# Holding weight splits back around two transposing stages of a decoder block, and moving the forget gate behind the first

## The chip, the core and the metric

The kernel runs on one core of a Trainium2 chip. The metric is the time of one execution on the device in microseconds, as the median of several runs. Traces come from one profiled execution on the same core.

## The reference

One hybrid decoder layer on 256 tokens of width 1024, in float32. Cut to its order:

```python
h = rms_norm(x, attn_norm_g)
qa, ka, va, qb, kb, vb, f_logit, g_logit = split(h @ w_in)     # 512 wide each, then 8, then 2048
qa, ka = partial_rope(rms_norm(heads(qa))), partial_rope(rms_norm(heads(ka)))
o_a = moba_attention(qa, ka, heads(va))       # 256 tokens are one block: causal softmax, 8 heads of 64
qb, kb = rms_norm(heads(qb)), rms_norm(heads(kb))
c = cumsum(log_sigmoid(f_logit + b_forget))   # the forget gate, one number per head and token
o_b = softmax(qb @ kb.T / 8 + c[t] - c[s], causal) @ heads(vb)
gates = sigmoid(g_logit + b_gate)
x = x + (gates[0] * (o_a @ w_branch_moba) + gates[1] * (o_b @ w_branch_fox)) @ w_out
u, g = split(rms_norm(x) @ w_ffn_up)
x = x + (silu(causal_conv(g)) * u) @ w_ffn_down
```

## The kernel before

**Split products.** Every large product is made of three: both operands are split into a high part in fp32r and a low part (value minus high part), and high x high, low x high and high x low are summed in one PSUM bank. Weights arrive in *chunks* of 128x2048 by one DMA each (L130, on SP's queue, into `raw`, three buffers) and are split in *halves* of 128x1024: the high part `whi` is a copy on ScalarE (L137), the low part `wlo` a subtraction on VectorE (L138). `whi` and `wlo` have six buffers each (`HB`). The raw buffer is free when the low part of its second half is made; a `whi`/`wlo` buffer is free when TensorE has used it.

**The order of the halves** is the list `units`: the eight `head` pieces (moba q and k), then "qkv" 1 (fox q, four halves), "qkv" 2 (fox k, four), "wg" 0 and 1 (two each), "qkv" 0 (moba v, four), "wg" 2, "qkv" 3 (fox v), "wg" 3 to 7, then "wb", "wo", "wu" and "wd". `use(c, h)` is called when TensorE's code comes to a half; it first emits the splits up to `AHEAD` = 5 halves further on (`load`), then hands out the half.

**What sets the order on the engines.** TensorE's order is the order of the code. On the other engines a planner orders instructions at compile time by its own picture of when each is ready and by a rank, which is the place in the code; inside `with soon(offset)` the rank is that many instructions earlier (`SOON` = 45, `FIRST` = 160). `after(i, j)` makes the planner put `i` behind `j`; on one engine this is an order alone, with no semaphore. PSUM has eight banks, taken by tile (`bank()`), and a bank is free when the instruction that reads it out is done.

**The two stages.** In TensorE's order:

1. `project(3)`, `project(4)` (fox q and fox k): 12 matmuls for each half. `finish_qk` follows each: squares on ScalarE (L308), sums per head on VectorE (L309), an inverse root in small steps (`rsqrt_mean`, L220 to L224, with two ScalarE steps at L221), and the scaling of q or k out of the bank (L321, one instruction for each 128 tokens).
2. `gate(0)`: 48 matmuls (L531 to L533) for one 128-wide column of both merge gates; VectorE takes it out of its bank (L541).
3. `turn_qk` four times (moba q, moba k, fox q, fox k): sixteen transposes each into two banks (L348), copied out by ScalarE (L353). `forget_a` stands ahead of the fourth: sixteen small products (L369), a high part on ScalarE (L370), a low part on VectorE (L371). `forget_b` sums its four strips by two more matmuls (L379) that stand behind the first three matmuls of the second half of `gate(1)`.
4. `gate(1)`, the moba scores and softmax, the moba v projection, `gate(2)`, the fox scores and softmax, the fox v projection, `gate(3)` to `gate(5)`.
5. `turn(0)` and `turn(1)`: 48 transposes each for the probabilities of the two branches (L483), into six banks each, copied out by six ScalarE copies each (L487). `last_exp[0]` is then the last of these twelve copies; the sigmoids of the gates (L545) are put behind it.
6. `gate(6)`, `values()` (probabilities times v, L501; copies of the result L517 and their low parts L518), `gate(7)`, then the branch products ("wb", L629 to L631), `w_out` and the feed-forward part.

Of the kernel before, what the change touches and what calls it, by code (L numbers as in the profile page):

```python
# [8 lines left out]
F32 = mybir.dt.float32  # L9
# [3 lines left out]
ALU = mybir.AluOpType  # L13
# [4 lines left out]
P = 128  # L18
S = 256
NT = 2  # L20
D = 1024
KT = D // P
HD = 64
NH = 8
# [6 lines left out]
RB, HB, AHEAD = 3, 6, 5  # L31
# [13 lines left out]
def decoder_block(ctx, tc, a, out):  # L45
    nc = tc.nc
# [6 lines left out]
    def T(shape, tag, bufs=1, dt=F32):  # L53
        return sb.tile(shape, dt, tag=tag, bufs=bufs, name=tag)
# [4 lines left out]
    def bank():  # L59
        return ps.tile([P, 512], F32, tag="bank", bufs=8, name="bank")  # L60
# [5 lines left out]
    def T16(n, tag, dt=F32R):  # L66
        t = T([P, n * S + 64], tag, 1, dt)
        return t[:, 4:4 + n * S].rearrange("p (k t) -> p k t", k=n)
# [24 lines left out]
    pos = {u: i for i, u in enumerate(units)}  # L93
# [1 line left out]
    loads = {}  # L95
    rs_done = []
    first_lo = []
    state = {"next": 0, "raw": None}

    def after(i, j):  # L100
        tc.add_manual_dep(i.ins, j.ins.name, mybir.DependencyInfo(mybir.DependencyClass.NoSync, mybir.DependencyReason.DATA), reason="order")

    def load(upto):
        while state["next"] <= min(upto, len(units) - 1):
            c, h = units[state["next"]]
            if c[0] == "head":
                k = c[1]
                if k < 2:
                    raw = gates[:, 4 * k:4 * k + 4].rearrange("p a b t -> p (a b t)")
                    for s0, s1 in ((0, HX + W4), (HX + W4, HEADW)):  # L110
                        loads[c] = nc.sync.dma_start(raw[:, s0:s1], a["head"][k][:, s0:s1])
                    x, g, raw = raw[:, 0:S], raw[:, S:S + 1], raw[:, HX:HEADW]
                    nc.gpsimd.tensor_copy(xT[:, k], x)
                else:
                    if k % 2 == 0:
                        state["raw"] = T([P, 2048], "raw", RB)
                    raw = state["raw"][:, k % 2 * 1024:(k % 2 + 1) * 1024]
                    x, g = xT[:, k], g1[:, k:k + 1]
                    nc.sync.dma_start(x, a["head"][k][:, 0:S])
                    loads[c] = nc.sync.dma_start(raw, a["head"][k][:, HX:HEADW])  # L120
                xlo = split_x(k, x, g)
                at, n = 44, 2 if k < 2 else 1
            else:
                at, n = 44 if c[0] == "qkv" else 0, 1
                if h == 0:
                    src = a[c[0]]
                    for j in c[1:]:
                        src = src[j]
                    state["raw"] = T([P, 2048], "raw", RB)
                    loads[c] = nc.sync.dma_start(state["raw"], src)  # L130
                raw = state["raw"][:, h * 1024:(h + 1) * 1024]
            hi = T([P, 1088], "whi", HB, F32R)[:, at:at + 1024]
            lo = T([P, 1088], "wlo", HB, F32R)[:, at:at + 1024]
            w = 1024 // n
            for j in range(n):
                s = slice(j * w, (j + 1) * w)
                i = nc.scalar.activation(hi[:, s], raw[:, s], AF.Copy)  # L137
                d = nc.vector.tensor_tensor(lo[:, s], raw[:, s], hi[:, s].bitcast(F32), op=ALU.subtract)  # L138
                if (c, h) == (("qkv", 1, 1), 0):
                    after(i, rs_done[0])  # L140
                    after(d, rs_done[1])
                if (c, h) == (("qkv", 1, 0), 0):
                    first_lo.append(d)
                if c[0] == "head" and j == 0:
                    after(d, xlo)
            if c[0] == "head":
                square_x(k, x, i)
            split[c, h] = (hi, lo)
            state["next"] += 1

    def use(c, h):
        load(min(pos[c, h] + AHEAD, KT + 1) if c[0] == "head" else pos[c, h] + AHEAD)
        return split.pop((c, h))


# [76 lines left out]
    flat = T16(4, "aT")  # L232
# [47 lines left out]
    def project(m, pt, h, between=None):  # L280
        for hh in range(2):
            if hh and between:
                between()
            wh, wl = use(("qkv", m - 2, h), hh)
            turns = [(k2, i, t) for k2 in range(2) for i in range(3) for t in range(NT)]
            if h == 0 and hh == 0:
                turns.sort(key=lambda x: x[2])
            for k2, i, t in turns:
                k = 4 * h + 2 * hh + k2
                c = slice(k2 * 512, (k2 + 1) * 512)  # L290
                lhs, rhs = ((xh, wh), (xl, wh), (xh, wl))[i]
                nc.tensor.matmul(pt[t], lhs[:, k, t * P:(t + 1) * P], rhs[:, c], start=(k == 0 and i == 0), stop=(k == KT - 1 and i == 2))  # L292
# [9 lines left out]
    def finish_qk(br, pts):  # L302
        n = len(pts)
        ss = T([P, 2, NT, NH], "ss", 2)[:, 0:n]
        for m, (isk, pt) in enumerate(pts):
            for t in range(NT):
                sq = T([P, W4], "sq", 2)
                nc.scalar.activation(sq, pt[t], AF.Square, scale=rs[:, t:t + 1])  # L308
                nc.vector.tensor_reduce(ss[:, m, t], sq.rearrange("p (h d) -> p h d", h=NH), axis=AX.X, op=ALU.add)  # L309
        f = T([P, 2, NT, NH], "qf", 2)[:, 0:n]  # L310
        rsqrt_mean(f.rearrange("p m t h -> p (m t h)"), ss.rearrange("p m t h -> p (m t h)"), HD, [n * NT * NH], "qfv")
        nc.vector.tensor_tensor(f, f, rs[:, None, :, None].to_broadcast([P, n, NT, NH]), op=ALU.mult)
        qns = []
        for m, (isk, pt) in enumerate(pts):
            if br == 0:
                qn = T([P, NT, NH, HD], "qn", 2)
            else:
                qn = qn1[:, 4 * isk:4 * isk + 4].rearrange("p k t -> p (k t)").rearrange("p (t h d) -> p t h d", t=NT, h=NH)
            qns.append(qn)
            for t in range(NT):  # L320
                nc.vector.tensor_tensor(qn[:, t], pt[t].rearrange("p (h d) -> p h d", h=NH),  # L321
                                        f[:, m, t, :, None].to_broadcast([P, NH, HD]), op=ALU.mult)
            if br == 0:
                rc, rsn = rope[isk]
                p1 = T([P, NT, NH, 16], "p1", 1)
                p2 = T([P, NT, NH, 16], "p2", 1)
                x16 = qn[:, :, :, 0:16]
                nc.gpsimd.tensor_tensor(p1, x16, rc[:, :, None, :].to_broadcast([P, NT, NH, 16]), op=ALU.mult)
                nc.gpsimd.tensor_tensor(p2, x16, rsn[:, :, None, :].to_broadcast([P, NT, NH, 16]), op=ALU.mult)
                nc.gpsimd.tensor_tensor(qn[:, :, :, 0:8], p1[:, :, :, 0:8], p2[:, :, :, 8:16], op=ALU.add)  # L330
                nc.gpsimd.tensor_tensor(qn[:, :, :, 8:16], p1[:, :, :, 8:16], p2[:, :, :, 0:8], op=ALU.add)
        return qns
# [32 lines left out]
    def forget_a():  # L365
        fp = bank()
        for k in range(KT):
            r = slice(32 * (k % 4), 32 * (k % 4 + 1))
            nc.tensor.matmul(fp[r, :S], wfg[:, k], xT[:, k], start=(k < 4), stop=(k >= 4))  # L369
        nc.scalar.activation(flat[:, 0], fp[:, :S], AF.Copy)  # L370
        nc.vector.tensor_tensor(flat[:, 1], fp[:, :S], flat[:, 0].bitcast(F32), op=ALU.subtract)  # L371

    def row(i):
        return gates[:NH, 4 + i // 2, i % 2]
# [51 lines left out]
    last_exp = []  # L426
# [110 lines left out]
    def gate(c, between=None):  # L537
        gp = bank()
        twin("wg", c, gp, xh, xl, between=between)
        with soon(FIRST):  # L540
            return nc.vector.tensor_tensor(gates[:, c], gp.rearrange("p (b t) -> p b t", b=2), rsB[:, None, :].to_broadcast([P, 2, S]), op=ALU.mult)  # L541
# [10 lines left out]
    def banks():  # L552
        return [bank() for _ in range(NT)]
# [11 lines left out]
        qkn = finish_qk(0, ((0, pq), (1, pk)))  # L565
    for isk in range(2):
        pt = banks()
        project(3 + isk, pt, 0)
        project(3 + isk, pt, 1)
        with soon(FIRST):  # L570
            qkn += finish_qk(1, ((isk, pt),))
    gate(0)
    with soon():
        for i, qn in enumerate(qkn):
            if i == 3:
                forget_a()
            turn_qk(qn, i // 2, i % 2)

    def between():
        with soon():  # L580
            forget_b()
# [21 lines left out]
    finish_v(pv, 1)  # L603
    gate(3)
    gate(4)
    gate(5)
    with soon():
        turn(0)
        last_exp[:] = [turn(1)]
    gate(6)  # L610
    oh, ol, copied = values()
    gate(7)
# [206 lines left out]
```

## Time and profile before

| | us |
|---|---|
| median of 3 runs | 366.54 (366.1 to 366.68) |
| the profiled execution | 364.58 |
| its span, first to last instruction | 362.8 |
| TensorE busy | 354.6 (98%) |
| VectorE busy | 274.4 (76%) |
| ScalarE busy | 218.0 (60%) |

In the profile PE is TensorE, PEld its weight loads, DVE VectorE, ACT ScalarE, POOL GpSimd, SP the engine whose queue issues the DMAs; L138 is line 138 of the kernel. A timeline row has start and duration in us, engine, line, operation, the tiles it writes and reads (out<-in), the shapes and how many instructions are merged in it; in brackets stands the idle time of the engine ahead of it, and what ended that idle time.

### The profile page before, as it was taken

To read this page: it belongs to the slowest core of one execution; us is meant where nothing else is said; L and a number is where in the kernel's file an instruction comes from. 1 tells how busy PE (TensorE), PEld (TensorE's weight loads), DVE (VectorE), ACT (ScalarE), POOL (GpSimd) and SP (SyncE) were. 2 spreads that over 40 slices of the span, in tenths; PEclk is the share of its full clock that TensorE was granted. 3 is DMA by queue.
4 is the path that set the end of the run, shared out by engine and by line. 5 is a ranking of instruction groups with operands and counts; after the bars stand their busy time and mean duration, and the time that the engine had idled before them with its cause. 6 is when DMAs were issued, how large, how long until landed. Compare 5 with 4: busy or idle time off the path is not lost.

```text
span 362.8 us, 7564 instructions
## 1 busy us (share of the span) xinstructions
PE 354.6 (98%) x3119; PEld 337.7 (93%) x3119; DVE 274.4 (76%) x483; ACT 218.0 (60%) x363; POOL 34.2 (9%) x51
## 2 busy tenths in 40 slices
PE   8999998999997999999999999999999999999995
PEld 5888897888897999999999999999999999999995
DVE  5899795899998267985979876768676866768643
ACT  5858657595695987544778545546455545546420
POOL 3432080320000000000530000000000000000000
PEclk9999999999999999999999999999999999999999
DMA  8987666326338433664555654554655554554003
GB/s 287 402 304 252 228 228 233 116 118 234 116 117 314 153 117 126 224 210 154 220 161 195 227 207 149 224 195 164 226 196 168 218 207 155 218 191 161 1 2 116
DMA packets 12131, 68.29 MB, mean 188 GB/s; under 512 B 1688, under 2 KB 2848, under 8 KB 4672
## 3 DMA queue, kind: packets, MB, share of 16 engines
q1 hardware_dynamic: 11664, 66.62, 51.1%
q0 software_dynamic: 288, 1.19, 0.8%
q8 instruction: 24, 0.39, 0.4%
q14 instruction: 11, 0.09, 0.1%
q10 hardware_dynamic: 144, 0.00, 0.0%
HBM read 66.75 MB, written 1.06 MB: 187 GB/s over the span
## 4 chain that ended last, share of the span: by engine, by line
PE 94%; DVE 2%; DMA 1%; issue 1%; ACT 1%; DVEq 0%
PE bank L531 15%; PE bank L533 15%; PE bank L532 14%; PE bank L292 12%; PE bank L278 6%; PE bank L733 6%; PE bank L732 5%; PE bank L731 5%; PE bank L657 2%; PE bank L631 2%; PE bank L656 2%; PE bank L655 2%; PE bank L630 2%; PE bank L629 2%; PE bank L501 1%; PE bank L440 1%
## 5 line engine op out<-in xcount | busy, mean ns | idle before, releaser
L138 DVE TENSOR_TENSOR wlo<-raw,whi 128x1024 fp32r<-128x1024 f32 x120 | 147.4, 1231 | 50.6 <-ACT whi L137 50.4
L137 ACT ACTIVATE whi<-raw 128x1024 fp32r<-128x1024 f32 x120 | 125.8, 1057 | 78.0 <-PE bank L532 42.0
L533 PE MATMUL bank<-oh,wlo 128*128 128x256 f32 x352 | 96.8, 275 | 0.0
L531 PE MATMUL bank<-oh,whi 128*128 128x256 f32 x352 | 96.8, 275 | 0.0
L532 PE MATMUL bank<-ol,whi 128*128 128x256 f32 x352 | 96.8, 275 | 0.0
L531 PEld LDWEIGHTS bank<-oh,whi 128*128 128x128 f32 x352 | 66.1, 188 | 0.0
L533 PEld LDWEIGHTS bank<-oh,wlo 128*128 128x128 f32 x352 | 66.1, 188 | 0.0
L532 PEld LDWEIGHTS bank<-ol,whi 128*128 128x128 f32 x352 | 66.1, 188 | 0.0
L531 PE MATMUL bank<-xh,whi 128*128 128x256 f32 x128 | 35.6, 278 | 0.0
L533 PE MATMUL bank<-xh,wlo 128*128 128x256 f32 x128 | 35.2, 275 | 0.0
L532 PE MATMUL bank<-xl,whi 128*128 128x256 f32 x128 | 35.2, 275 | 0.0
L531 PEld LDWEIGHTS bank<-xh,whi 128*128 128x128 f32 x128 | 24.0, 188 | 0.3
L532 PEld LDWEIGHTS bank<-xl,whi 128*128 128x128 f32 x128 | 24.0, 188 | 0.1
L533 PEld LDWEIGHTS bank<-xh,wlo 128*128 128x128 f32 x128 | 24.0, 188 | 0.0
L292 PE MATMUL bank<-whi,xh 128*128 128x512 f32 x64 | 21.2, 391 | 0.0
L292 PE MATMUL bank<-whi,xl 128*128 128x512 f32 x64 | 21.0, 388 | 0.0
L292 PE MATMUL bank<-wlo,xh 128*128 128x512 f32 x64 | 21.0, 388 | 0.0
L698 DVE TENSOR_TENSOR sq<-bank,rs 128x512 f32<-128x512 f32 x22 | 15.1, 691 | 6.6 <-PE bank L533 6.5
L629 PE MATMUL bank<-oh,whi 128*128 128x256 f32 x64 | 17.6, 275 | 0.0
L630 PE MATMUL bank<-ol,whi 128*128 128x256 f32 x64 | 17.6, 275 | 0.0
L631 PE MATMUL bank<-oh,wlo 128*128 128x256 f32 x64 | 17.6, 275 | 0.0
L655 PE MATMUL bank<-xh,whi 128*128 128x256 f32 x64 | 17.6, 275 | 0.0
(200 smaller groups left out, 749.5 us busy)
## 6 DMA issues: line engine op xcount, KB each, us to landing
raw<-in_wu SPq DMA_DIRECT2D x22, 1024.0 KB, 4.8
raw<-in_wd SPq DMA_DIRECT2D x11, 1024.0 KB, 4.8
raw<-in_qkv SPq DMA_DIRECT2D x8, 1024.0 KB, 4.9
raw<-in_wg SPq DMA_DIRECT2D x8, 1024.0 KB, 4.8
raw<-in_wb SPq DMA_DIRECT2D x4, 1024.0 KB, 5.3
raw<-in_wo SPq DMA_DIRECT2D x4, 1024.0 KB, 4.9
raw<-in_head SPq DMA_DIRECT2D x6, 512.0 KB, 6.6
gates<-cd POOLq DMA_DIRECT2D x1, 1024.0 KB, 4.5
```

The lines of the kernel that those rows point to most:

```text
L137: i = nc.scalar.activation(hi[:, s], raw[:, s], AF.Copy)
L138: d = nc.vector.tensor_tensor(lo[:, s], raw[:, s], hi[:, s].bitcast(F32), op=ALU.subtract)
L278: nc.tensor.matmul(pt[t], lhs[:, k, t * P:(t + 1) * P], rhs, start=(k == 0 and i == 0), stop=(k == KT - 1 and i == 2))
L292: nc.tensor.matmul(pt[t], lhs[:, k, t * P:(t + 1) * P], rhs[:, c], start=(k == 0 and i == 0), stop=(k == KT - 1 and i == 2))
L531: nc.tensor.matmul(o, wh[:, w], mh[:, k], start=(k == 0 and i == 0), stop=False)
L532: nc.tensor.matmul(o, wh[:, w], ml[:, k], start=False, stop=False)
L533: nc.tensor.matmul(o, wl[:, w], mh[:, k], start=False, stop=(k == KT - 1 and i == 1))
L629: nc.tensor.matmul(o, wh[:, w], oh[:, 4 * br + k], start=(k == 0), stop=False)
L630: nc.tensor.matmul(o, wh[:, w], ol[:, 4 * br + k], start=False, stop=False)
L631: nc.tensor.matmul(o, wl[:, w], oh[:, 4 * br + k], start=False, stop=(k == 3))
L655: nc.tensor.matmul(o, wh[:, w], mh[:, k], start=(k == 0 and i == 0), stop=False)
L733: nc.tensor.matmul(o, wl[:, w], ah, start=False, stop=(last and h == 1 and d == ds[-1]))
```

## The change

`state` gains a `lag`: for halves behind the `head` pieces `use` emits splits up to `AHEAD - lag` halves further on. `catch_up(lag, hi, lo)` sets a new lag and at once emits the halves that the smaller lag allows (one half at each of its three calls); `hi` and `lo` name instructions behind which the high and the low parts of these halves are put. The lag is 2 in `project(4)`; behind it one half is emitted with its low part behind k's last scaling (L321), and the lag is 1 through `gate(0)`. `forget_a` moves behind the fourth `turn_qk`; behind it one half is emitted with its low part behind the forget gate's low part (L371), and the lag is 0. In `gate(5)` the lag is 1 again; behind `turn(1)` one half is emitted with its high part behind the last copy of the turned probabilities (L487). No instruction is added or removed.

```diff
-    state = {"next": 0, "raw": None}
+    state = {"next": 0, "raw": None, "lag": 0, "hi": None, "lo": None}
...
                 if c[0] == "head" and j == 0:
                     after(d, xlo)
+                for this, last in ((i, state["hi"]), (d, state["lo"])):
+                    if last is not None:
+                        after(this, last)
...
+    def catch_up(lag=0, hi=None, lo=None):
+        upto = state["next"] - 1 + state["lag"] - lag
+        state.update(lag=lag, hi=hi, lo=lo)
+        load(upto)
+        state.update(hi=None, lo=None)
+
     def use(c, h):
-        load(min(pos[c, h] + AHEAD, KT + 1) if c[0] == "head" else pos[c, h] + AHEAD)
+        load(min(pos[c, h] + AHEAD, KT + 1) if c[0] == "head" else pos[c, h] + AHEAD - state["lag"])
...
-                nc.vector.tensor_tensor(qn[:, t], pt[t].rearrange("p (h d) -> p h d", h=NH),
-                                        f[:, m, t, :, None].to_broadcast([P, NH, HD]), op=ALU.mult)
+                state["qn"] = nc.vector.tensor_tensor(qn[:, t], pt[t].rearrange("p (h d) -> p h d", h=NH),
+                                                      f[:, m, t, :, None].to_broadcast([P, NH, HD]), op=ALU.mult)
...
-        nc.vector.tensor_tensor(flat[:, 1], fp[:, :S], flat[:, 0].bitcast(F32), op=ALU.subtract)
+        return nc.vector.tensor_tensor(flat[:, 1], fp[:, :S], flat[:, 0].bitcast(F32), op=ALU.subtract)
...
         pt = banks()
+        state["lag"] = 2 * isk
         project(3 + isk, pt, 0)
         project(3 + isk, pt, 1)
         with soon(FIRST):
             qkn += finish_qk(1, ((isk, pt),))
+    catch_up(lag=1, lo=state["qn"])
     gate(0)
     with soon():
         for i, qn in enumerate(qkn):
-            if i == 3:
-                forget_a()
             turn_qk(qn, i // 2, i % 2)
+        flat_lo = forget_a()
+    catch_up(lo=flat_lo)
...
     gate(4)
+    state["lag"] = 1
     gate(5)
     with soon():
         turn(0)
         last_exp[:] = [turn(1)]
+    catch_up(hi=last_exp[0])
     gate(6)
```

## The prediction

> **What bounds the kernel now.** I read the page's summary, then TensorE's own waits, then the timelines of TensorE, VectorE and ScalarE around each wait, and one piece of the chain that ended last.
>
> ```profile
> span 362.8 us, 7564 instructions
> PE 354.6 (98%) x3119; PEld 337.7 (93%) x3119; DVE 274.4 (76%) x483; ACT 218.0 (60%) x363; POOL 34.2 (9%) x51
> ```
>
> TensorE is busy 354.6 of 362.8 us. The change takes no matmul away, so all it can win is idle TensorE time, 8.2 us at most. Who ends that idle time (columns: total us, times, longest):
>
> ```profile
> PE bank L483 <- DVE gates L541: 1.9, 1, 1.9
> PE bank L348 <- DVE gates L541: 0.7, 1, 0.7
> PE bank L348 <- DVE ol L321: 0.4, 1, 0.4
> ```
>
> All three stand at transposes: L483 turns the probabilities, L348 turns q and k. VectorE ends them: twice by L541, which empties a gate's bank, once by L321, which scales k. The first stage on TensorE (start us, us):
>
> ```profile
> 54.17 1.21 PE L348 MATMUL bank<-cst,qn 64*128 64x64 f32 x32
> 55.22 0.22 PE L348 MATMUL bank<-cst,ol 64*128 64x64 f32 x1
> 56.17 0.71 PE L348 MATMUL bank<-cst,ol 64*128 64x64 f32 x15 [0.72 <-DVE gates L541]
> 56.80 1.07 PE L369 MATMUL bank<-xT,wfg 128*32 128x256 f32 x16
> 58.29 0.97 PE L348 MATMUL bank<-cst,ol 64*128 64x64 f32 x16 [0.41 <-DVE ol L321]
> 59.19 0.38 PE L531 MATMUL bank<-xh,whi 128*128 128x256 f32 x1
> ```
>
> From 54.17 to gate(1)'s first matmul at 59.19 pass 5.02 us. The work in it: 32 transposes start within 1.05 us (54.17 to 55.22), so 64 take 2.10, and the forget gate's sixteen products (L369) take 1.07. That is 3.17; the other 1.85 us are waits, some of them inside the rows of x15 and x16. VectorE at that time, with one ScalarE row (52.84):
>
> ```profile
> 48.60 1.25 DVE L138 TENSOR_TENSOR wlo<-raw,whi 128x1024 fp32r<-128x1024 f32 x1
> 50.05 1.28 DVE L309 TENSOR_REDUCE ss<-sq 128x8 f32<-128x512 f32 x2 [0.19 <-ACT sq L308]
> 51.24 1.22 DVE L138 TENSOR_TENSOR wlo<-raw,whi 128x1024 fp32r<-128x1024 f32 x1
> 52.84 0.46 ACT L221 ACTIVATE qfv<-qfv 128x16 f32<-128x16 f32 x2 [0.33 <-DVE qfv L220]
> 52.73 1.21 DVE L138 TENSOR_TENSOR wlo<-raw,whi 128x1024 fp32r<-128x1024 f32 x1
> 54.21 1.21 DVE L138 TENSOR_TENSOR wlo<-raw,whi 128x1024 fp32r<-128x1024 f32 x1
> 55.43 0.68 DVE L541 TENSOR_TENSOR gates<-bank,rsB 128x512 f32<-128x512 f32 x1
> 56.12 1.21 DVE L138 TENSOR_TENSOR wlo<-raw,whi 128x1024 fp32r<-128x1024 f32 x1
> 57.45 1.29 DVE L321 TENSOR_TENSOR ol<-bank,qf 128x512 f32<-128x512 f32 x2
> 62.83 0.41 DVE L380 TENSOR_TENSOR gates<-bank,rsB 8x256 f32<-8x256 f32 x1 [3.40 <-PE bank L379]
> ```
>
> Between k's sum of squares (L309, over at 51.33) and k's scaling (L321, 57.45) four weight splits lie in line, 4.85 us. They are the halves of the moba v projection, which comes behind gate(1). Later VectorE sits idle 3.40 us. The second stage, TensorE first (its last row, at 124.85, is from the chain that ended last), then VectorE, ScalarE and the DMA queue:
>
> ```profile
> 113.19 0.28 PE L533 MATMUL bank<-xh,wlo 128*128 128x256 f32 x1
> 113.53 0.28 PE L533 MATMUL bank<-xh,wlo 128*128 128x256 f32 x1
> 113.73 1.72 PE L483 MATMUL bank<-cst,s 64*128 64x64 f32 x48
> 115.29 0.22 PE L483 MATMUL bank<-cst,ol 64*128 64x64 f32 x1
> 117.44 0.96 PE L483 MATMUL bank<-cst,ol 64*128 64x64 f32 x23 [1.92 <-DVE gates L541]
> 119.11 0.39 PE L531 MATMUL bank<-xh,whi 128*128 128x256 f32 x1
> 124.85 4.85 PE bank L501 x160
> 108.06 4.62 DVE L138 TENSOR_TENSOR wlo<-raw,whi 128x1024 fp32r<-128x1024 f32 x4
> 113.20 1.21 DVE L138 TENSOR_TENSOR wlo<-raw,whi 128x1024 fp32r<-128x1024 f32 x1
> 115.56 1.23 DVE L138 TENSOR_TENSOR wlo<-raw,whi 128x1024 fp32r<-128x1024 f32 x1 [1.14 <-ACT whi L137]
> 116.70 0.68 DVE L541 TENSOR_TENSOR gates<-bank,rsB 128x512 f32<-128x512 f32 x1
> 114.46 2.00 ACT L137 ACTIVATE whi<-raw 128x1024 fp32r<-128x1024 f32 x2 [4.22 <-PE bank L483]
> 116.37 3.02 ACT L487 ACTIVATE pT<-bank 128x512 f32<-128x512 f32 x6
> 131.14 2.02 ACT L517 ACTIVATE oh<-bank 128x512 fp32r<-128x512 f32 x4
> 109.34 9.53 SPq L130 DMA_DIRECT2D raw<-in_wb  x4
> ```
>
> Gate(5) is done at 113.73, but L541 empties its bank only at 116.70: in front of it stands the low part of the first "wb" half (115.56), which waits for its high part (114.46). The trace names L483 as what ended ScalarE's 4.22 us; I read it as the chunk's DMA, issued at 109.34, 5.12 us earlier. That half is used only behind gate(6), the products with v (L501, over at 129.70) and gate(7). It also holds up the copies of the turned probabilities (116.37). The rows at 113.19 and 113.53 are three matmuls apart: 0.113 us each, 5.44 for a gate's 48.
>
> **The change part by part.** *Lag 2 and the first held half.* With lag 2 in k's projection and lag 1 in gate(0), each half is emitted one or two turns later. By itself that only lowers its rank. The hold is in `catch_up`: the low part at 48.60 (second half of "wg1") goes behind the last L321. If the halves behind it keep their turn, all four splits of the table leave the chain. What then remains: L309 ends at 51.33; to ScalarE and back (L221, 0.46, with a hand-over on each side) about 1.0; four short steps at some 0.1 each; L321 from about 52.8 to 54.1. The transposes that need it come after 54.17 + 48 x 0.033 = 55.75, so they don't wait, and even one split of 1.21 left in the chain would do no harm. L541 can start when gate(0) ends, about 54.1, and is over by 55.0; the third set of transposes needs its bank at 55.22.
>
> *Forget gate behind all turning.* Its 1.07 us covered part of the wait for L321. With L321 early there is nothing to cover, and the move costs nothing; with L321 as late as now it costs up to those 1.07. Then gate(1) starts at 54.17 + 3.17 = 57.34 instead of 59.19: **1.85 us**. The forget gate's low part (L371) follows behind a ScalarE copy of its bank, done by about 58.8; its consumer on TensorE stands 27 matmuls into gate(1), at about 60.4. The half held by L321 is used 24 matmuls into gate(1), at 60.1, and done by about 56.0. The halves behind L371 are wanted only when gate(1) is through, after 62.8, and the 3.40 us of idle VectorE take them in. Holding a low part also holds its raw buffer, so on SP's queue the chunks from "wg2" on are asked for some 5 us later; TensorE takes "wg2" a whole projection after gate(1), so nothing waits. I take **1.8**; ends: 1.85, and a loss of 1.1 (L321 as late as now, cover gone).
>
> *Lag 1 at gate(5).* The first "wb" half leaves ScalarE's and VectorE's line in front of L541 and the copies. VectorE then ends the split of 113.20 at 114.41, L541 runs to 115.1, and the 49th transpose, ready at 115.29, finds its bank. Copies of 0.50 each (3.02 for six) start once sixteen transposes are through, at about 114.3, and free a pair of banks at 115.3 and 116.3; the second half of the turning needs them at about 115.85 and 116.4. So that stage ends 1.9 us earlier, just in time at each bank. Part may go back: ScalarE has no idle time from 114.46 until L517 has copied the attention's result (131.14 to 133.16), and the two splits moved behind the copies still lie ahead of L517. TensorE would want branch 0 of that result at 129.70 + 5.44 - 1.9 = 133.2; its two copies end at 132.2, which leaves 1.0 for two low parts on VectorE. I let 0.2 go there and take **1.7**; ends: 1.9, and 0 (the next half of the same chunk takes the empty place).
>
> [...] The clock row (columns: PE, PEld, DVE, ACT, POOL busy, PEclk, DMA share, GB/s):
>
> ```profile
> 72.00:109.00 37.00, 37.00 (x294) 33.52 (x293) 35.26 (x120) 28.80 (x73) 1.92 (x6) 1.00 0.41 148
> 113.80:119.10 5.30, 3.38 (x97) 3.18 (x96) 3.57 (x4) 4.64 (x8) 0.00 (x0) 1.00 0.92 373
> 119.10:124.90 5.80, 5.80 (x55) 5.67 (x54) 0.00 (x0) 5.77 (x11) 0.00 (x0) 1.00 0.48 181
> ```
>
> The granted clock is 1.00 throughout the turning and in gate(6) behind it. [...]
>
> **Sum.** 1.8 + 1.7 = 3.5 us. The profiled execution (span 362.8, time 364.58) would go to 359.3 and 361.1. The median of the three runs is 366.54, 1.96 above the profiled time; I take the saving from it: 363.0.
>
> **Rivals.** *Overtaking: the halves behind a held one don't wait for it.* Only named halves are held. At the copies the other half of the same chunk could take the place of the held one, with the same late DMA, and L541 waits again: 366.5 - 1.8 = 364.7. At k's scaling three halves are left free to fill the chain; three leave L321 at about 57.6, where the early scaling and the lost cover cancel: with both, 366.5. Against it: a hold of this kind exists in the kernel already (the third half of the fox q weights, behind the first norm), and there the next half of the same chunk did not slip in, though ScalarE idled:
>
> ```profile
> 26.29 0.44 ACT L221 ACTIVATE rsv<-rsv 128x2 f32<-128x2 f32 x2 [3.07 <-DVE rsv L220]
> ```
>
> *Only one stage gains, for another reason*, such as L541 kept late by some other step, or L517's end ruling: 364.7 or 364.8.
>
> *Slower: held splits land in the crowded stretch.* From 72 to 109 VectorE is busy 35.26 of 37.00 us. Gate(5)'s second half is split at 108.06, over by 109.3, and used at 111.0 (24 x 0.113 ahead of 113.73): some 1.7 us to spare, the least of all. If the halves behind L371 miss the idle 3.40 us and come behind the softmax, each pushes the later splits back by 1.2 us. TensorE, 1.8 early, then stands at gate(5). With all five halves (6.1 us) the wait is 6.1 - 1.7 = 4.4, the sum 366.5 - 3.5 + 4.4 = 367.4; it decides from 1.7 + 3.5 = 5.2 us on. For it: L371 waits for work that now comes last in its stage. [...] Against it: the gap comes first.
>
> [...]
>
> **How the numbers follow.** Both stages gain: 0.56 (362.5 to 364.0, likeliest 363.0). One stage: 0.22 (about 364.7). Nothing, by overtaking in both: 0.12 (about 366.5). Slower: 0.09 (about 367.4). Clock: 0.01. A measurement here can tell about 0.2%, 0.73 us, from no change. Faster 0.79, same 0.12, slower 0.09. The range takes in the first two cases, with 0.8 below the likeliest for what I can't see and up to 365.6 for a stage that gains half: 362.2 to 365.6.
>
> **What would show it.** Right: no wait of L483 or L348 for L541 or L321 beyond some 0.2 us; k's L321 over before 55.8; gate(1) 3.2 us and gate(6) 3.3 us after the turning's first transpose; the copies L487 starting within 0.7 us of it; the first "wb" split behind the twelfth copy. Wrong: low parts between L309 and L321 (overtaking), TensorE waiting for whi or wlo at gate(3) to gate(5) (crowded stretch), or for oh at L629 (L517's end rules).

## The result and the profile after

The median went from 366.36 us (six runs, 364.75 to 366.68) to 362.56 (six, 362.08 to 363.14): 0.9902 of the time before, 95% interval 0.9883 to 0.9922. The forecast of 363.0 is near it. The way there was another one: two errors of the forecast, 1.4 and 1.7 us, nearly cancel. Two executions are left out of all figures, one of before (447.88 us, clock 0.756) and one of the kernel with eight more matmuls (373.01, 0.95).

The profiled execution of after, the longest of its six, took 363.14 us at a mean granted clock of 0.999. Lines after the change stand nine further down: L348 is L357, L369 is L378, L371 is L380, L380 is L389, L321 is L330, L483 is L492, L541 is L550. Its summary, then TensorE's waits (without one of 0.8 us at the very start, which before has too):

```profile
span 361.4 us, 7561 instructions
PE 355.3 (98%) x3119; PEld 338.1 (94%) x3119; DVE 273.8 (76%) x483; ACT 217.7 (60%) x363; POOL 31.5 (9%) x51
...
PE bank L301 <- DVE gates L550: 0.8, 1, 0.8
PE bank L492 <- DVE gates L550: 0.5, 1, 0.5
```

Of the three waits of before, those in the first stage are gone, that at the probabilities shrank from 1.9 to 0.5, and a new one of 0.8 stands at L301, the fox v projection. Both that are left are for a gate's bank. TensorE's timeline of the two stages, and the new wait between them:

```profile
54.62 1.21 PE L357 MATMUL bank<-cst,qn 64*128 64x64 f32 x32
55.66 1.16 PE L357 MATMUL bank<-cst,ol 64*128 64x64 f32 x32
56.75 1.07 PE L378 MATMUL bank<-xT,wfg 128*32 128x256 f32 x16
57.75 0.39 PE L540 MATMUL bank<-xh,whi 128*128 128x256 f32 x1
...
87.42 0.50 PE L301 MATMUL bank<-whi,xh 128*128 128x512 f32 x1 [0.77 <-DVE gates L550]
...
113.78 1.72 PE L492 MATMUL bank<-cst,s 64*128 64x64 f32 x48
115.33 0.22 PE L492 MATMUL bank<-cst,ol 64*128 64x64 f32 x1
116.09 0.96 PE L492 MATMUL bank<-cst,ol 64*128 64x64 f32 x23 [0.53 <-DVE gates L550]
116.83 0.97 PE L492 MATMUL bank<-cst,qn 64*128 64x64 f32 x24
117.72 0.39 PE L540 MATMUL bank<-xh,whi 128*128 128x256 f32 x1
```

The first stage takes 57.75 - 54.62 = 3.13 us (5.02 before), the second 117.72 - 113.78 = 3.94 (5.38 before). That makes 3.3 us. Between the stages TensorE gives back 1.49, by the starts of its projections and gates against the same starts before: 0.14 from gate(1) to the scores, 1.21 in the fox v projection, where the wait of 0.77 stands, and 0.14 in gate(3) to gate(5). TensorE's products also ran 0.44 late from before the first changed instruction on (the fox q projection starts at 27.31 instead of 26.87). So this execution is 3.3 - 1.49 - 0.44 = 1.4 us shorter than the one profiled before: 363.14 against 364.58.

Where that came from is on VectorE, ScalarE and SP's queue. Rows of after:

```profile
50.48 1.28 DVE L318 TENSOR_REDUCE ss<-sq 128x8 f32<-128x512 f32 x2 [1.37 <-ACT sq L317]
...
54.14 1.29 DVE L330 TENSOR_TENSOR ol<-bank,qf 128x512 f32<-128x512 f32 x2
55.35 0.68 DVE L550 TENSOR_TENSOR gates<-bank,rsB 128x512 f32<-128x512 f32 x1
55.95 3.49 DVE L138 TENSOR_TENSOR wlo<-raw,whi 128x1024 fp32r<-128x1024 f32 x3
60.60 0.42 DVE L380 TENSOR_TENSOR aT<-bank,aT 128x256 fp32r<-128x256 f32 x1 [1.16 <-ACT aT L379]
60.94 2.35 DVE L138 TENSOR_TENSOR wlo<-raw,whi 128x1024 fp32r<-128x1024 f32 x2
63.21 0.41 DVE L389 TENSOR_TENSOR gates<-bank,rsB 8x256 f32<-8x256 f32 x1
...
69.35 0.58 DVE L454 MEMSET bank<- 64x128 f32 x4
...
63.16 1.06 ACT L137 ACTIVATE whi<-raw 128x1024 fp32r<-128x1024 f32 x1 [2.59 <-DMA raw<-in_wg]
64.12 0.49 ACT L394 ACTIVATE gates<-gates,sm 8x256 f32<-8x256 f32 x1
...
57.23 0.33 SPq L130 DMA_DIRECT2D raw<-in_wg  x1
```

and the same places before:

```profile
68.32 0.58 DVE L445 MEMSET bank<- 64x128 f32 x4
...
63.28 0.51 ACT L385 ACTIVATE gates<-gates,sm 8x256 f32<-8x256 f32 x1
...
49.88 0.33 SPq L130 DMA_DIRECT2D raw<-in_wg  x1
```

No split lies between k's sum of squares and k's scaling any more. But "wg2" is asked for at 57.23 instead of 49.88, because the held low part keeps its raw buffer. ScalarE waits 2.59 us for that chunk, and the forget gate's chain (L394), which needs nothing of it, stands behind in ScalarE's order. VectorE's first step of the moba softmax (L454) comes at 69.35 instead of 68.32, while TensorE is early. From 72 to 109 VectorE is busy for 35.26 of 37.00 us (before), so it has little room to make this up. SP's queue shows it: the first "wb" chunk is asked for at 110.36 instead of 109.34, later by 1.02 us where the softmax was later by 1.03. What VectorE does late TensorE waits for at its next banks.

**Two groups of times.** In the batches below, 79 executions of the kernel before have their clock on record. 31 of them took 364.5 to 365.3 us (median 364.70) at a mean clock of 0.998 to 1.0; 48 took 365.8 to 366.9 (median 366.57) at 0.994 or 0.995, and nothing lies between. The execution profiled before (364.58, 0.999) is of the lower group, while five of the six runs behind the median of 366.36 took 366.1 or more. All six runs of after have a clock of 0.998 or more. So the 3.8 us between the medians are 364.70 - 362.56 = 2.1 of waits and 366.36 - 364.70 = 1.7 that go with the clock.

### The profile page after: what moved, and what is told of

It reads as the page before. It is cut to its first block, busy times and chain, and to the rows that moved or that the text cites. A ratio compares the mean times of both kernels' runs of the same rounds, so it can differ in the third digit from the quotient of the medians.

```text
span 361.4 us, 7561 instructions
## 1 busy us (share of the span) xinstructions
PE 355.3 (98%) x3119; PEld 338.1 (94%) x3119; DVE 273.8 (76%) x483; ACT 217.7 (60%) x363; POOL 31.5 (9%) x51
## 4 chain that ended last, share of the span: by engine, by line
PE 83%; DVE 6%; ACT 6%; DMA 2%; issue 1%; ACTq 0%
PE bank L540 13%; PE bank L541 13%; PE bank L542 13%; PE bank L301 8%; PE bank L287 6%; PE bank L745 6%; PE bank L746 6%; PE bank L744 6%; DVE wlo L138 3%; PE bank L670 2%; PE bank L644 2%; PE bank L669 2%; PE bank L668 2%; PE bank L643 2%; PE bank L642 2%; ACT whi L137 2%
## 5 line engine op out<-in xcount | busy, mean ns | idle before, releaser
L541 PE MATMUL bank<-ol,whi 128*128 128x256 f32 x352 | 96.8, 275 | 0.0
L541 PEld LDWEIGHTS bank<-ol,whi 128*128 128x128 f32 x352 | 66.1, 188 | 0.0
L541 PE MATMUL bank<-xl,whi 128*128 128x256 f32 x128 | 35.3, 276 | 0.0
L541 PEld LDWEIGHTS bank<-xl,whi 128*128 128x128 f32 x128 | 24.0, 188 | 0.1
L301 PE MATMUL bank<-whi,xh 128*128 128x512 f32 x64 | 21.3, 393 | 0.8 <-DVE gates L550 0.8
L301 PE MATMUL bank<-whi,xl 128*128 128x512 f32 x64 | 21.0, 388 | 0.0
L301 PE MATMUL bank<-wlo,xh 128*128 128x512 f32 x64 | 21.0, 388 | 0.0
```

Source lines behind the costliest of these rows:

```text
L541: nc.tensor.matmul(o, wh[:, w], ml[:, k], start=False, stop=False)
```

## The experiments

Ratios are to the kernel before in runs of the same batch, with their 95% intervals.

**Each stage alone.** First stage only: the lag and the hold at gate(5) are left out.

```diff
     gate(4)
-    state["lag"] = 1
     gate(5)
...
-    catch_up(hi=last_exp[0])
```

> The first stage's part alone: lag 2, the two holds and the forget gate behind all turning; gate(5) and the turning of the probabilities as before. Theory (both stages gain, and the first gives part of it back later because VectorE runs late): from the first q/k transpose to gate(1) 3.1 us (5.02 before), then a wait of about 1 us at the fox v projection for gate(2)'s read-out, and the turning of the probabilities at 5.4 us or more as before; 365.0 to 366.2 against 366.4 before. Rival (nothing is given back): 364.5. Rival (the whole gain is in the first stage): 362.6.

Measured: 367.25 us (365.68 to 368.89), ratio 1.0046 (1.0026 to 1.0067): slower than before. The rows of TensorE and VectorE, and the windows of the turning and of the 3.41 us after 118.29 (columns as in the prediction's clock rows):

```profile
117.96 1.33 PE L492 MATMUL bank<-cst,ol 64*128 64x64 f32 x23 [2.83 <-DVE gates L550]
...
116.08 1.23 DVE L138 TENSOR_TENSOR wlo<-raw,whi 128x1024 fp32r<-128x1024 f32 x1 [1.08 <-ACT whi L137]
117.22 0.68 DVE L550 TENSOR_TENSOR gates<-bank,rsB 128x512 f32<-128x512 f32 x1
...
113.36:118.29 4.93, 2.10 (x60) 1.97 (x61) 3.85 (x5) 3.30 (x5) 0.00 (x0) 1.00 0.99 404
118.29:121.70 3.41, 3.41 (x50) 3.29 (x45) 0.75 (x1) 3.41 (x9) 0.00 (x0) 0.50 0.75 228
```

Two things happen. L550 still waits behind the first "wb" half, and TensorE comes 0.4 us sooner (the turning starts at 113.36), the chunk 0.6 us later (asked for at 109.93 instead of 109.34), by as much as the softmax is late here too (68.94 instead of 68.32). The wait at L492 grows from 1.9 to 2.8, and the first stage's gain is gone before gate(6). And the granted clock falls to 0.50 for 3.41 us. All twelve runs show 0.995 or less, four of them 0.991, which would be two such falls; one costs up to 3.41/2 = 1.7 us, an estimate from its length and its clock.

Second stage only: the first stage as before, with the forget gate in its old place.

```diff
-        state["lag"] = 2 * isk
...
-    catch_up(lag=1, lo=state["qn"])
...
+            if i == 3:
+                flat_lo = forget_a()
             turn_qk(qn, i // 2, i % 2)
-        flat_lo = forget_a()
-    catch_up(lo=flat_lo)
```

> The second stage's part alone: lag 1 at gate(5) and the first wb half behind the last copy. Theory: from the first transpose of the probabilities to gate(6) 3.3 to 3.9 us (5.38 before), the first stage at 5.0; 364.5 to 364.9. Rival (the whole gain is in the second stage): 362.6. Rival (the second half of the wb chunk takes the empty place): 366.4.

Measured: 362.91 (362.7 to 363.46), ratio 0.9923 (0.99 to 0.9945). The turning of the probabilities and gate(6) behind it:

```profile
113.85 1.72 PE L492 MATMUL bank<-cst,s 64*128 64x64 f32 x48
117.36 0.39 PE L540 MATMUL bank<-xh,whi 128*128 128x256 f32 x1
```

The turning takes 3.5 us, with no wait in it, all clocks are 0.997 or more, and the first stage keeps its waits of 0.7 and 0.4. Against the lower group of before it wins 364.70 - 362.91 = 1.8. Most of what the change brings is brought by this stage alone.

**The parts of the first stage.** The forget gate back ahead of the fourth turn, all else as after:

```diff
+            if i == 3:
+                flat_lo = forget_a()
             turn_qk(qn, i // 2, i % 2)
-        flat_lo = forget_a()
```

> The changed kernel with the forget gate's products back in front of the fourth set of transposes. Theory (with k's scaling early there is nothing to cover, the move is worth nothing): first stage 3.1 to 3.3 us, the time that of the changed kernel, 362.2 to 363.0. Rival (the move itself is part of the gain): first stage 3.6 to 4.2 us, 363.1 to 363.6.

Measured: 363.54 (362.87 to 363.98), ratio 0.9937 (0.9913 to 0.996). The stage itself takes 3.28 us instead of 3.13 (54.58 to 57.86). The rest of the 1 us to after (362.40 and 362.56, in other batches) is not explained: in its profiled execution "wg2" is copied 6.1 us after it is asked for (5.9 and 5.2 in the two traces of after), ScalarE waits 2.78 for it, and TensorE 0.9 at L301. What the place of the forget gate is worth stays open between 0.15 and 1 us.

The lags without the orders (no `lo`, no `hi`):

```diff
-    catch_up(lag=1, lo=state["qn"])
+    catch_up(lag=1)
...
-    catch_up(lo=flat_lo)
+    catch_up()
...
-    catch_up(hi=last_exp[0])
+    catch_up()
```

> The changed kernel without the three orders (nothing is put behind k's scaling, the forget gate's low part or the copies); lags and the move of the forget gate stay. Theory (a lag lowers a rank and holds nothing; the forget gate's cover is lost): first stage 6.0 to 6.2 us, turning of the probabilities 5.4 us; 367.0 to 367.8, slower than before. Rival (the lag does the work): 362.6.

Measured: 367.92 (366.02 to 369.23), ratio 1.0053 (1.0031 to 1.0075). TensorE in its first stage, then windows in and behind both:

```profile
56.19 0.71 PE L357 MATMUL bank<-cst,ol 64*128 64x64 f32 x15 [0.72 <-DVE gates L550]
58.31 1.11 PE L357 MATMUL bank<-cst,ol 64*128 64x64 f32 x16 [1.41 <-DVE ol L330]
59.35 1.93 PE L378 MATMUL bank<-xT,wfg 128*32 128x256 f32 x16
...
58.96:62.37 3.41, 3.41 (x29) 2.02 (x28) 0.42 (x1) 1.65 (x3) 0.00 (x0) 0.50 0.71 293
120.40:123.81 3.41, 3.41 (x45) 3.29 (x42) 0.61 (x1) 3.41 (x9) 0.00 (x0) 0.50 0.69 240
```

A later place in the code holds nothing: VectorE makes the splits ahead of the scaling all the same (four of 1.21 to 1.22 between 51.26 and 57.34; the scaling starts at 57.47). The order edges do the holding. The forget gate's 1.07 us no longer cover the wait (1.41 us instead of 0.41), which is what the prediction priced. In this execution the clock fell behind both stages; two of the twelve runs, 366.0 and 366.2, show no fall, six of them two (368.1 to 369.2).

**The late chunk and the late forget gate.** Three kernels and after once more; the second was run in another batch than the others. The first holds the *first* half of the next chunk instead of the second of "wg1", so that its raw buffer comes free:

```diff
-        state["lag"] = 2 * isk
+        state["lag"] = isk
...
-    catch_up(lag=1, lo=state["qn"])
+    catch_up(lo=state["qn"])
+    state["lag"] = 1
```

> The changed kernel with the first hold one half later: lag 1 instead of 2 in k's projection, so that the second half of wg1 is split in VectorE's gap ahead of k's sums, and the first half of the moba v weights is held behind k's scaling instead. Theory (the changed kernel gives back most of its first stage because two things start VectorE's next stage late: wg1's raw buffer comes free 7 us later, so wg2's load lands late and ScalarE waits 2.6 us for it in front of the forget gate's steps; and two splits stand in front of L389): the wait for wg2 goes, L389 stays where it is, 0.4 us won against the changed kernel of the same batch, about 362.1. Rival (the load is the whole cause): VectorE's scores start 1 us earlier, 1.0 to 1.5 us won, about 361.2. Rival (neither matters): no difference.

The second takes the order behind the forget gate's low part away:

```diff
-    catch_up(lo=flat_lo)
+    catch_up()
```

> The changed kernel with its first hold, but the half that was put behind the forget gate's low part is put behind nothing: five splits then stand in front of L380, and L389 follows L380 at once. Theory (both the late load of wg2 and the two splits in front of L389 keep VectorE's scores late; taking one away alone wins little): the five splits end at about 61.7, TensorE waits about 1 us for L380 in gate(1), ScalarE still waits for wg2 until about 62.4; 362.0 to 362.8, no more than 0.4 us from the changed kernel. Rival (the place of L389 is the whole cause): about 361.3, as the run with both changes.

The third does both:

> As the run with the hold one half later, and the half that was put behind the forget gate's low part is put behind nothing, so that all splits stand in front of L380 and L389 follows it at once. Theory: L389 starts at about 61.2 instead of 63.2 and the forget gate's steps on ScalarE 2 us earlier; the wait of 0.8 us at the fox v projection and the wait of 0.5 us at the turning of the probabilities go; 1.3 to 1.6 us won against the changed kernel, about 361.0. Rival (late VectorE is not what costs): as the changed kernel, 362.5.

After itself, without an edit:

> The changed kernel once more, for a second trace and a comparison in the same batch. [...] The waits of the first trace (0.8 us at the fox v projection, 0.5 us at the probabilities) come again if they belong to the kernel, and not if that execution was an odd one.

Measured: the first 362.26 (ratio 0.9897, 0.9874 to 0.992), the second 362.14 (0.9912, 0.9887 to 0.9938), both together **361.24** (0.9872, 0.9849 to 0.9895), after 362.40 (0.9907, 0.9883 to 0.9932). What L394, the forget gate's chain on ScalarE, stands behind, and when the softmax starts, in the first of them:

```profile
63.46 0.51 ACT L394 ACTIVATE gates<-gates,sm 8x256 f32<-8x256 f32 x1 [1.69 <-DVE gates L389]
...
68.44 0.58 DVE L454 MEMSET bank<- 64x128 f32 x4
```

in the second:

```profile
62.08 1.06 ACT L137 ACTIVATE whi<-raw 128x1024 fp32r<-128x1024 f32 x1 [1.90 <-DMA raw<-in_wg]
63.04 0.49 ACT L394 ACTIVATE gates<-gates,sm 8x256 f32<-8x256 f32 x1
...
68.25 0.58 DVE L454 MEMSET bank<- 64x128 f32 x4
...
61.71 0.39 PE L388 MATMUL bank<-aT 128*128 128x256 f32 x1 [0.84 <-DVE aT L380]
```

and in both together, with the turning of the probabilities:

```profile
62.27 0.51 ACT L394 ACTIVATE gates<-gates,sm 8x256 f32<-8x256 f32 x1
...
67.31 0.58 DVE L454 MEMSET bank<- 64x128 f32 x4
...
112.74 1.72 PE L492 MATMUL bank<-cst,s 64*128 64x64 f32 x48
114.29 0.92 PE L492 MATMUL bank<-cst,ol 64*128 64x64 f32 x24
115.04 1.28 PE L492 MATMUL bank<-cst,qn 64*128 64x64 f32 x24
116.25 0.39 PE L540 MATMUL bank<-xh,whi 128*128 128x256 f32 x1
```

L394 has two things ahead of it: the late chunk on its own engine, and on VectorE the two splits in front of L389, which the order behind the low part puts there. Take one away and the other ends the wait. Counted from the first transpose of the first stage, L394 starts after 9.50 and 9.03 us in the two traces of after, after 9.04 and 8.81 with one gone, and after 7.43 with both gone. In the second kernel the splits that now stand in front of the forget gate's low part (L380) cost TensorE 0.84 at L388 instead. With both gone the softmax follows, the "wb" chunk is asked for at 108.33, no wait at L301 or L492 is left, and the turning takes 3.5 us. Against the lower group of before the change so mended wins 364.70 - 361.24 = 3.5 us. It beats both kernels: all of its six runs (360.95 to 361.69) lie below those of after in the same batch (362.2 to 363.57).

**The clock.** Four kernels test what makes it fall. First, the kernel before with eight ordinary matmuls (128x512, bf16, into banks that are overwritten behind them) among the transposes:

```diff
         for g in range(24):
+            if (br, g) in ((0, 16), (1, 8)):
+                for _ in range(4):
+                    nc.tensor.matmul(tps[g // 8][0], warm[:, 0:P], warm, start=True, stop=True)
```

> The kernel before with eight extra matmuls of the warm-up's kind (128x512, bf16) among the transposes of the probabilities, four after the first 16 and four after the first 56, written to a bank that the transposes then overwrite; nothing else is moved. The kernel before has two groups of times, 364.5 to 365.0 at a mean clock of 0.999 and 366.0 to 366.9 at 0.995. [...]

Measured: 366.09, ratio 0.9997 (0.9982 to 1.0012). Its eleven runs lie in one group, 365.73 to 366.34, at clocks of 0.998 or more: the fall is gone, and the matmuls cost 1.4 us against before's lower group. But they also break up the transposing and fill idle time (the wait at the transposes is 0.8 instead of 1.9), so this doesn't tell which of the two brought the fall. Next, the second stage alone with each of the 96 transposes issued twice:

```diff
-            for h, r in enumerate(halves):
+            for h, r in 2 * tuple(enumerate(halves)):
```

> The second stage's part alone, with each of the 96 transposes of the probabilities issued twice (the second one writes the same again). The turning, 3.5 us and without a wait in the second stage's part alone, becomes about 6.8 us in which TensorE is busy with transposes throughout. [...] Rival (only idle time lets the clock fall): every run at 0.998 or more, 366.2.

Measured: 366.63 (366.29 to 367.63), ratio 1.0031 (1.0014 to 1.0048), every one of the twelve clocks 0.998 or more. It is not the transposing that brings the fall, as the windows of the turning and of the 3.41 us behind it show:

```profile
114.30:120.89 6.59, 6.35 (x193) 6.21 (x192) 1.27 (x2) 5.09 (x10) 0.00 (x0) 1.00 0.74 301
120.89:124.30 3.41, 3.41 (x32) 3.41 (x30) 1.29 (x2) 3.35 (x5) 0.00 (x0) 1.00 0.02 5
```

6.59 us of transposes and nothing else on TensorE, and the clock behind them is 1.00. What is left is the idle time. So the last two fill the wait with the first 48 transposes issued a second time, in the kernel before:

```diff
-            for h, r in enumerate(halves):
+            for h, r in (2 - br) * tuple(enumerate(halves)):
```

> The kernel before, with the first 48 of the 96 transposes of the probabilities issued twice (1.6 us, by 0.033 each), so that TensorE transposes on while it would wait for the gate's bank (1.92). Theory, as it stands after the doubled turning: the clock falls in those executions in which TensorE's idle time in the turning, not the transposing, leaves too little work in a stretch of 3.4 us. Then the wait shrinks from 1.9 to about 0.3, nothing gets later, no run shows a mean clock under 0.998, and all runs form one group at 364.5 to 365.4: about 364.9. [...]

and in the kernel with the first stage alone:

> The first stage's part of the change alone (367.25, every run at a clock of 0.995 or less, wait of 2.8 us at the probabilities' transposes), again with the first 48 transposes of the probabilities issued twice. Theory (idle time lets the clock fall): the wait goes from 2.8 to about 1.25, less than the 1.9 with which the kernel before drops in two of three runs; the clock stays at 0.998 or more in most runs, and the time is about 1.8 below that of the first stage's part alone: 365.0 to 365.6. If a wait of 1.25 still lets the clock fall in some runs, two groups are 1.8 apart. [...]

Measured: 364.76 (364.44 to 365.42), ratio 0.9973 (0.9956 to 0.999), and 364.88 (364.55 to 365.41), ratio 0.998 (0.9963 to 0.9997); all 24 clocks are 0.997 or more. The wait in the first, then in the second:

```profile
117.36 0.96 PE L483 MATMUL bank<-cst,ol 64*128 64x64 f32 x23 [0.48 <-DVE gates L541]
```

```profile
118.06 0.96 PE L492 MATMUL bank<-cst,ol 64*128 64x64 f32 x23 [1.52 <-DVE gates L550]
```

48 more transposes, which do nothing, make the first stage's kernel 367.25 - 364.88 = 2.4 us faster, and put the kernel before into its lower group whole (364.76 against 364.70). In order of the longest wait in the turning, each as its one profiled execution shows it: at 1.52 us none of 12 runs shows a fall, at 1.92 (before, in an execution without a fall) 48 of 79, at 2.83 all 12. It is not the longest gap alone: in the kernel with the lags only, 0.72 and 1.41 us of waiting with sixteen transposes between them were followed by a fall (a wait of 1.89 stands ahead of its second). What the falls have in common is how little TensorE did in the 3.41 us ahead of them. The windows ahead of the fall in the first stage alone, of both falls with the lags only, and the emptiest such stretch of the turning in the first stage's kernel with the wait filled, which never falls:

```profile
114.88:118.29 3.41, 0.58 (x18) 0.45 (x15) 2.33 (x4) 3.30 (x5) 0.00 (x0) 1.00 0.99 394
55.55:58.96 3.41, 1.32 (x27) 1.08 (x29) 3.17 (x6) 3.16 (x6) 0.00 (x0) 1.00 0.86 308
116.99:120.40 3.41, 1.52 (x47) 1.38 (x45) 2.35 (x3) 3.41 (x6) 0.00 (x0) 1.00 0.98 401
114.65:118.06 3.41, 1.89 (x61) 1.76 (x57) 2.15 (x4) 2.98 (x5) 0.00 (x0) 1.00 0.99 396
```

TensorE was busy for 0.58, 1.32 and 1.52 of 3.41 us ahead of the falls, and for 1.89 where none came. The profiled execution of before has 1.49 in its emptiest stretch and no fall, so this figure alone does not decide it; what does is not shown.

That the first stage alone gains nothing, seen in the profile of its kernel, is also seen without the clock: 364.88 against 364.70.

## Why the prediction was right, point by point

- *The hold.* Right. Nothing overtakes a held half: no split stands between L318 and L330 in after, and the first "wb" half is copied behind the twelfth copy. The lags without the orders show that the orders do it, as "by itself that only lowers its rank" had it.
- *First stage, 1.8.* Right in its place: 3.13 us against 3.17 forecast, k's scaling over at 55.43. Moving the forget gate cost nothing there (3.28 with it in its old place).
- *"TensorE takes 'wg2' a whole projection after gate(1), so nothing waits."* This step failed. The wait is ScalarE's: 2.59 us in front of the forget gate's chain, and from there VectorE's softmax is late. I had priced the late chunk by its user on TensorE alone, and not by what stands behind its split on ScalarE; it was also asked for 7.35 us later (57.23 against 49.88) where I had said some 5. "The 3.40 us of idle VectorE take them in" failed in part: two of the splits stand in front of L389. Together these took back 1.49 us in the profiled execution, and 0.76 (0.14, 0.50 and 0.12) in a second one of after; with both mended it is 0.05.
- *Second stage, 1.7.* The mechanism was right, the size 5.38 - 3.94 = 1.44. The 0.2 that I took off for L517 didn't show; what did is 0.53 at the 50th transpose, because gate(5)'s bank is emptied behind a split that VectorE, late since the softmax, makes only at 114.22. The mended kernel shows 1.87 there. It is the "crowded stretch" rival at a small scale: gate(5)'s second half has 0.7 us to spare in after, where it had 1.6. Two of the signs named for "right" therefore stayed away: the wait of 0.53 is above 0.2, and gate(6) starts 3.94 us after the turning's first transpose and not 3.3. By the sum itself that should have read 5.38 - 1.9 = 3.5, which the mended kernel takes.
- *The stages as a sum.* They don't add singly: the first alone is worth 0, the second 1.8. As I read it, the gain of the first reaches the end only if the second stage's bank is no longer tied to a chunk's arrival; the first stage alone with the softmax mended was not run, so this is not shown. The change does both, so the sum could hold, and in the mended kernel it does: 3.5 us.
- *"I take the saving from it", and the 0.01 for the clock.* This step failed by about as much as the other, the other way. The granted clock of 1.00 in the turning and in gate(6) was true for its execution, one of the 31 without a fall. The 1.96 us between the median and the profiled time were the fall in the others (1.9 us between the two groups). I saw that difference and carried it along as a constant. The fall is what took the median 1.7 us further down: with the wait in the turning filled, all twelve runs of the kernel before stay at 0.997 or more, at a median of 364.76. How much one fall can cost follows from the length and the clock of those that a trace caught (3.41 us at 0.50): 3.41/2 = 1.7, an estimate.

So the working would have given 364.7 - 3.5 = 361.2 by the profiled group; it was 362.56, 1.4 more, and the fall, 1.7 us that the sum did not hold, made the median's move look like the forecast. That the number came out this close is luck; that both stages shrink is not.

## What to carry to other kernels

When a split is held back, ask what its input buffer is needed for next: here it was better to hold the first half of the next chunk than the last of this one. Look at every engine that takes the late chunk in order, not only at the one that uses it in the end. A place later in the code does not hold an instruction that a planner may put into a gap; an order does. And before a profiled time is set against a median, lay out the single runs with their clocks: a gap of 2 us between the two was here a group of executions that the trace did not show.

## What the runs showed of the hardware

In the turning of 5.4 us, with a wait of 1.9 us for a bank, the mean clock of an execution was down to 0.994 or 0.995 in 48 of 79 executions; with a wait of 2.8 it was at 0.995 or less in all 12, with one of 1.5 at 0.997 or more in all 12. Where a trace caught a fall, the granted clock was 0.50 for 3.41 us, and TensorE had been busy for at most 1.52 of the 3.41 us ahead of it. One such fall thus costs up to 3.41/2 = 1.7 us, an estimate from these two numbers. Transposes of 64x64 in f32 that do nothing, at 0.033 us each (32 start within 1.05 us), kept the clock at 0.997 or more in all 24 runs of the two kernels that drop, in some or all executions, without them. Doubled, 6.59 us of them with nothing else on TensorE were followed by a clock of 1.00.
